# First layer's experts: the last three groups added on TensorE, rows fetched earlier, the branch for left-over rows at the head

## The chip, the cores and the metric

The kernel runs on one core of a Trainium2 chip. The metric is device microseconds of one execution; times are compared as medians of several runs, and the trace is of one further, profiled execution.

## What is computed

Two layers of a small diffusion backbone on 256 context tokens and 256 latent tokens of width 1024. Each layer has a mixer (pooling and differential attention) and then a hierarchical mixture of 32 experts. The change lies in the experts of the first layer, which run over all 512 tokens, and where the second layer's mixer begins. Of the reference that is:

```python
probs_c = jax.nn.softmax(t @ rc_w + rc_b)            # one of four groups for each token
top_v, top_i = lax.top_k(lf, TOP_K_FINE)             # two of its eight experts
gates = einsum('nk,nke->ne', softmax(top_v) * p_group, one_hot(expert_id, N_EXPERTS))
hid = silu(t @ w_gate) * (t @ w_up) * gates          # for each expert
out = sum over the experts of hid @ w_down
x = x + g2 * out                                     # likewise for the context tokens
# the next layer begins with: hx = rmsnorm(x, norm1_g) * (1 + sc1) + sh1;  px = hx @ w_in
```

## The kernel before, in words

**Groups.** A token's row is sent only to its two experts. Experts are sorted by their number of rows, and the sorted list is cut into blocks of 32 rows; four blocks make a group of 128 rows. The first layer has 15 groups, 0 to 14 (`N` and `G` are 15 there). Group 12, 13 and 14 hold four experts each. For every group, `step_apart` runs: `up` (gate and up products, L1445), `turn_hid`, `down` (L1479), and for later groups in between `table` (which rows they take, and a gather of these rows by POOL, L1247) and `turn` (transposes).

**Results of a group.** Group 0 to 12 are "apart" (L1214): the 128 result rows go through `yring` to a table `YD` in memory by a scatter on POOL's queue (L1489). Group 13 and 14 are added on TensorE instead: a selection matrix `P` times the results' high and low parts (`yh`, `yl`; L1529, L1530), one 128 x 512 sum per token tile and half, which `add` multiplies by the gate vector (DVE, L1505) and adds to X (L1507, by DVE and POOL in turn for group 13, by DVE for group 14). The rows in `YD` come back by `fetch` (POOL's queue, L1512, two rows a token, 1 MB a tile) and are added by `add_rows` (three DVE instructions of 128 x 1024, L1517 to L1519). Tiles 0 and 1 are fetched behind group 12, tiles 2 and 3 behind group 13, when the first two have been added.

**Slots and loads.** SBUF has 19 slots of 1 MB (`SB`), used for weights and for large tiles alike. An expert has three loads of 1 MB, issued by SP in one order. Each load in the experts' part takes the slot that `give` hands back when a product has read its weights; `join` takes all slots that lie free into this ring; a load into such a fresh slot is unconditional, every other one is left out by the hardware if the expert has no rows. `lend` hands slots back to `SB` instead. What the next layer loads waits in `pending`; `pump` issues it whenever a slot comes free and more than `keep` stay free. If a request finds no slot, `fill_any` runs a waiting piece of work, here one unit of the modulation matrix of the next layer (`ada_unit`, four matmuls, L414), and takes its slot.

**The branch.** If an expert has more rows than its blocks hold, `left_over` computes them in a loop behind a branch (L1562, L1563). All engines read the flag and branch. Before the change it stands behind group 7. It needs two slots, which `lend` provides. In the runs shown it isn't taken.

**The end of the layer.** `at_end` and `tile_done` begin the next layer's norm for tiles 0 and 1 as their sums are done. The first weight of the next layer has two halves, each split into a high part (ACT) and a low part: the first half's low part by POOL (L500), the second half's by DVE in `mixer`. There `prepare(t)` transposes a tile's rows (L533), scales and splits them (L546 to L551), and the product of each tile follows (L597), copied out by ACT (L599).

## Time and profile before

| | us |
|---|---|
| median of the runs shown | 970.52 (968.68 to 973.1) |
| the profiled execution, its own time | 971.53 |
| its span on the core | 969.7 |
| TensorE matmul busy | 809.7 (84%) |
| VectorE (DVE) busy | 440.9 (45%) |
| ScalarE (ACT) busy | 264.4 (27%) |
| GpSimd (POOL) busy | 189.4 (20%) |
| moved by DMA | 292.91 MB, mean 302 GB/s |

The span is from the first to the last instruction of the trace; what lies around it is 1.8 us here. Matmuls are pipelined, so TensorE's busy time counts overlaps and slow matmuls as busy. Busy time is an average over stages with different limits: the first layer's experts run from some 290 to 590 us, the second layer's mixer follows to some 770, and its experts to the end.

### The profile page before, as it was taken

Reading aid. Unit: us, or ns where it says so; the run is one execution under the profiler, and the core shown is the slowest. Engines: PE = TensorE matmul, PEld = TensorE weight load, DVE = VectorE, ACT = ScalarE, POOL = GpSimd, SP = SyncE. Lnnn points to the kernel's source line nnn. Section 1 sums busy time; section 2 is a strip of 40 time slices with the busy share of each in tenths; the row PEclk is TensorE's granted clock in tenths of the full one; section 3 lists DMA queues with packets and bytes.
Section 4 is the critical chain, followed back from the end, with each engine's and each line's share of the span. In section 5 each row is a group of like instructions: output and inputs, shape, how many; then the busy total and the mean of one; then the engine's idle time right before and its main releaser. Section 6 shows DMA issues by size and latency. Waiting matters only on the chain.

```text
span 969.7 us, 13386 instructions
## 1 busy us (share of the span) xinstructions
PE 809.7 (84%) x4825; PEld 438.2 (45%) x4825; DVE 440.9 (45%) x956; ACT 264.4 (27%) x592; POOL 189.4 (20%) x201
## 2 busy tenths in 40 slices
PE   4799999988995789989866765899878689999873
PEld 1467765654784233333221122677556534443311
DVE  0534405576476222232111078644675734766533
ACT  1632216345350111111000004632572311111101
POOL 1400002234611111111100024000126211222211
PEclk9799999999997889999999887899999789999987
DMA  9988388820729999997999992473227689999992
GB/s 377 417 350 320 130 342 312 332 88 7 303 75 361 369 369 416 416 418 314 410 419 418 408 401 113 179 300 130 97 99 267 249 311 418 418 418 416 418 400 77
DMA packets 49081, 292.91 MB, mean 302 GB/s; under 512 B 7571, under 2 KB 7955, under 8 KB 16880
## 3 DMA queue, kind: packets, MB, share of 16 engines
q1 hardware_dynamic: 36864, 265.74, 68.2%
q0 software_dynamic: 6336, 13.99, 3.8%
q10 hardware_dynamic: 5808, 12.25, 3.4%
q8 instruction: 41, 0.67, 0.3%
q14 instruction: 32, 0.26, 0.1%
HBM read 317.29 MB, written 15.30 MB: 343 GB/s over the span
## 4 chain that ended last, share of the span: by engine, by line
PE 24%; DMA 16%; DVE 6%; ACT 3%; POOL 2%; issue 2%; SPq 0%; POOLq 0%; DVEq 0%; ACTq 0%
DMA we<-in_wx_dram 16%; PE gu L1445 7%; PE dn L1479 5%; PE pj L597 2%; PE pj L467 2%; PE pj L469 2%; PE pj L468 2%; DVE m L1505 1%; PE rowps L414 1%; POOL wl L500 1%; DVE o L1228 1%; POOL wl L464 1%; PE hTp L1264 1%; DVE mx L712 1%; ACT e L718 1%
## 5 line engine op out<-in xcount | busy, mean ns | idle before, releaser
L1479 PE MATMUL dn<-we,t 128*32 128x512 f32 (+2 forms) x672 | 108.5, 639 | 6.5 <-DMA we<-in_wx_dram 4.8
L1451 DVE SCALAR_TENSOR_TENSOR t<-t,tb,gu 128x256 f32<-128x256 f32 x25 | 12.0, 480 | 190.4 <-ACT t L1450 190.4
L1445 PE MATMUL gu<-we,hT0modh 128*32 128x512 f32 (+1 forms) x400 | 62.9, 629 | 10.5 <-DMA we<-in_wx_dram 8.6
L1450 ACT ACTIVATE t<-gu 128x256 f32<-128x256 f32 x25 | 9.6, 384 | 227.0 <-PE gu L1445 227.0
L1445 PE MATMUL gu<-we,hT0modl 128*32 128x512 f32 (+1 forms) x400 | 61.6, 594 | 10.7 <-DMA we<-in_wx_dram 10.1
L1479 PEld LDWEIGHTS dn<-we,t 128*32 128x32 f32 (+2 forms) x672 | 29.5, 122 | 67.6 <-issue 55.0
L414 PE MATMUL rowps<-ada,sT 128*32 128x512 f32 x384 | 54.3, 653 | 5.1 <-DMA ada<-in_adaw_dram 5.1
L1507 POOL TENSOR_TENSOR X<-X,m 128x512 f32<-128x512 f32 x24 | 30.7, 1277 | 142.0 <-DVE m L1505 141.8
L1445 PE MATMUL gu<-we,hT1modl 128*32 128x512 f32 (+1 forms) x272 | 45.6, 652 | 6.1 <-DMA we<-in_wx_dram 6.1
L467 PE MATMUL pj<-hH,wh 128*128 128x512 f32 (+1 forms) x128 | 47.6, 372 | 0.0
L468 PE MATMUL pj<-hL,wh 128*128 128x512 f32 (+1 forms) x128 | 46.5, 363 | 0.0
L469 PE MATMUL pj<-hH,wl 128*128 128x512 f32 (+1 forms) x128 | 46.5, 363 | 0.0
L1507 DVE TENSOR_TENSOR X<-X,m 128x512 f32<-128x512 f32 x32 | 43.6, 1363 | 1.1
L718 ACT ACTIVATE e<-S,nb 128x512 f32<-128x512 f32 (+1 forms) x48 | 29.2, 613 | 46.9 <-DVE nb L715 31.7
L1445 PE MATMUL gu<-we,hT1modh 128*32 128x512 f32 (+1 forms) x272 | 39.5, 622 | 2.4 <-DMA we<-in_wx_dram 1.4
L1247 POOL DMA_INDIRECT h<-hd,ix x14 | 14.3, 1021 | 134.9 <-DVE iy L1254 62.6
L1445 PEld LDWEIGHTS gu<-we,hT0modh 128*32 128x32 f32 (+1 forms) x400 | 17.0, 121 | 52.2 <-issue 35.4
L1445 PEld LDWEIGHTS gu<-we,hT0modl 128*32 128x32 f32 (+1 forms) x400 | 17.0, 115 | 51.1 <-issue 34.2
L712 DVE TENSOR_REDUCE mx<-S 128x1 f32<-128x512 f32 (+1 forms) x48 | 26.8, 596 | 27.7 <-PE S L710 27.6
L1505 DVE TENSOR_TENSOR m<-cb,g 128x512 f32<-128x512 f32 x56 | 36.4, 680 | 0.1
L751 PE MATMUL o<-v,t 128*128 128x128 f32 x160 | 24.5, 293 | 10.3 <-ACT t L739 10.3
L751 PEld LDWEIGHTS o<-v,t 128*128 128x128 f32 x160 | 20.1, 194 | 26.3 <-ACT t L739 23.7
(336 smaller groups left out, 1580.8 us busy)
## 6 DMA issues: line engine op xcount, KB each, us to landing
we<-in_wx_dram SPq DMA_DIRECT2D x207, 1024.0 KB
ada<-in_adaw_dram SPq DMA_DIRECT2D x48, 1024.0 KB
YD<-m ACTq DMA_DIRECT2D x1, 4096.0 KB
yb<-YD POOLq DMA_DIRECT2D x4, 1024.0 KB, 13.5
X<-in_x_dram SPq DMA_DIRECT2D x4, 512.0 KB
e<-in_modb_dram ACTq DMA_DIRECT2D x8, 256.0 KB
band<-in_band_dram SPq DMA_DIRECT2D x2, 1024.0 KB
hd<-h ACTq DMA_DIRECT2D x4, 512.0 KB
```

Of the source, the lines that this page charges most:

```text
L414: pe.matmul(rowps[l][32 * j:32 * j + 32], lhsT=sT[:, k, 4 - 2 * cb:36 - 2 * cb], rhs=h.t[:, 512 * j:512 * j + 512], start=cb < 2 and k == ...
L467: pe.matmul(ps, lhsT=lh, rhs=rh, start=first, stop=False)
L468: pe.matmul(ps, lhsT=lh, rhs=rl, start=False, stop=False)
L469: pe.matmul(ps, lhsT=ll, rhs=rh, start=False, stop=last)
L597: pe.matmul(p.t, lhsT=H[kh].t[:, k, ts], rhs=W3[kh][part].t[:, k], start=n == 0, stop=n == 23)
L712: dve.reduce_max(mx[:, m:m + 1], p.t[:, :nk], axis=AX.X)
L718: act.activation(e[m][:, :nk], S[m].t[:, :nk], AF.Exp, scale=0.125, bias=nb[:, m:m + 1], accum_out=l_[:, m:m + 1])
L751: pe.matmul(o.t[:, h], lhsT=aT[:, kt], rhs=v.t[:, kt, h * 128:h * 128 + 128], start=kt == 0, stop=kt == n - 1)
L1445: pe.matmul(p.t[r], lhsT=hT[k // 4][:, k % 4, r], rhs=gate_up(weights(w, k // 4), k), start=k == 0, stop=k == 7)
L1479: pe.matmul(ps[n2].t[r], lhsT=aT[:, k, r], rhs=down_w(weights(w, 2), k, n2), start=k == 0, stop=k == 1)
L1505: tt(m, q, self.g2[stream(t)][:, ns], op=OP.mult)
L1507: e.tensor_tensor(X[:, t, ns], X[:, t, ns], m, op=OP.add)
```

## The change

The branch `left_over` moves from behind group 7 to the head, ahead of group 0; one slot is kept out of the first `join`, so that it finds two. Group 12 is no longer sent through `YD` but added on TensorE right behind its down product, all by DVE. All four tiles' rows are fetched behind group 11, into three lent slots and `yring`; tiles 0 and 1 are added behind group 12, tiles 2 and 3 behind group 13. The results of groups 13 and 14 are held (`yy`, two slots), and `combine_last` adds both in one sum of four matmuls for each tile and half: tiles 0 and 1 at the layer's end, tiles 2 and 3 inside the next layer's `mixer`, as `late(2)` and `late(3)`. The first half of the next layer's first weight is split ahead of group 14's down product, by ACT and DVE; the second half is copied by ACT ahead of the sums. The loads of the next layer may use every free slot from group 11 on.

```diff
@@ -550,7 +550,7 @@
-    def mixer(l, W3, rows, pre):
+    def mixer(l, W3, rows, pre, late=None):
         last = l == NL - 1
@@ -577,13 +577,15 @@
         else:
-            rests[2]()
+            late(2)
             rests[1](dve)
...
                 prepare(t + 1)
+            if t == 0 and late:
+                late(3)
             if t == 2:
@@ -1203,7 +1205,7 @@
             G = len(groups)
-            tabs, hid, ys, pick = {}, {}, {}, {}
+            tabs, hid, ys, pick, held = {}, {}, {}, {}, []
             hgs = SB.get([128, 2, D], F32, "hg") if near else self.rings.pop(0)
@@ -1211,7 +1213,7 @@
-            apart = lambda g: not near and g < N - 2
+            apart = lambda g: not near and g < N - 3
             rows, back = {}, {}
@@ -1229,7 +1231,7 @@
                 if picked(g):
-                    pick[g] = both[:, 256:].rearrange("p (t s) -> p t s", t=2) if near else w2("e").rearrange("p (t s) -> p t s", t=4)
+                    pick[g] = both[:, 256:].rearrange("p (t s) -> p t s", t=2) if near else yring.t[:, 1, 0:512].rearrange("p (t s) -> p t s", t=4)
                     tt(pick[g], ohs[0][:, :T], ohs[1][:, :T], op=OP.add)
@@ -1364,10 +1366,10 @@
-            def join():
+            def join(left=0):
...
                 hold, SB.after = SB.after, None
-                while SB.slots:
+                while len(SB.slots) > left:
                     h = SB.get([128, 2048], F32, "we")
@@ -1379,7 +1381,7 @@
                 early[0] = 0
-                join()
+                join(1 if N == G else 0)
@@ -1466,8 +1468,9 @@
                 nr = rows_of(g)
+                aside = not near and g >= N - 2
                 if not apart(g):
-                    P = w2("e", F32R)
+                    P = w2("o" if aside and g == N - 2 else "e", F32R)
                     dve.tensor_scalar(P[:nr, :nt], iota512[:nr, :nt], tabs[g][:nr, 6:7], None, op0=OP.is_equal)
@@ -1489,14 +1492,20 @@
                     return
+                for d_ in done:
+                    give(d_, 2)
+                if aside:
+                    hold, SB.after = SB.after, None
+                    if g == N - 2:
+                        hgs.free()
+                    held.append(SB.get([128, 4, 512], F32R, "yy"))
+                    SB.after = hold
                 for n2 in range(2):
-                    yh.append(w2("e", F32R))
-                    yl.append(w2("e", F32R))
+                    yh.append(held[-1].t[:, 2 * n2] if aside else w2("e", F32R))
+                    yl.append(held[-1].t[:, 2 * n2 + 1] if aside else w2("e", F32R))
                     act.activation(yh[n2][:nr], ps[n2].t[:nr], AF.Copy)
...
                     ps[n2].free()
-                for d_ in done:
-                    give(d_, 2)
                 ys[g] = (P, yh, yl)
@@ -1519,7 +1528,7 @@
-            def combine(g, part, tile_done=None):
+            def combine(g, part, tile_done=None, e=None):
                 P, yh, yl = ys[g] if part == 0 else ys.pop(g)
@@ -1528,10 +1537,23 @@
                         pe.matmul(q.t, lhsT=lt, rhs=yl[n2][:nr], start=False, stop=True)
-                        add(q.t, i, n2, None if near or tile_done is None else dve)
+                        add(q.t, i, n2, e)
                         q.free()
...
                         tile_done(i)
+
+            def combine_last(i):
+
+                for n2 in range(2):
+                    q = PS.get([128, 512], F32, "cb")
+                    for n, g in enumerate((N - 2, N - 1)):
+                        P, yh, yl = ys[g]
+                        nr = rows_of(g)
+                        lt = P[:nr, i * 128:i * 128 + 128]
+                        pe.matmul(q.t, lhsT=lt, rhs=yh[n2][:nr], start=n == 0, stop=False)
+                        pe.matmul(q.t, lhsT=lt, rhs=yl[n2][:nr], start=False, stop=n == 1)
+                    add(q.t, i, n2, dve)
+                    q.free()
@@ -1554,9 +1576,6 @@
             gp.dma_start(gv.rearrange("(t p) e -> p t e", p=128), go)
-            room.free()
-            join()
-
             def left_over():
@@ -1609,6 +1628,13 @@
+            hold, SB.after = SB.after, None
+            room.free()
+            if N == G:
+                left_over()
+            SB.after = hold
+            join()
+
             def step_apart(g):
@@ -1637,20 +1663,25 @@
                     turn(g + 1, 1)
+                if g == N - 1 and tail:
+                    tail()
                 down(g)
+                if g == N - 4:
+                    yring.free()
+                    for i in range(T):
+                        fetch(i)
+                    keep[0] = 0
                 if g == N - 3:
-                    for i in range(2):
-                        fetch(i)
-                if g == N - 2:
-                    hgs.free()
                     for part in range(2):
-                        combine(g, part)
+                        combine(g, part, None, dve)
+                    hold, SB.after = SB.after, None
                     for i in range(2):
                         add_rows(i)
+                    SB.after = hold
+                    join()
+                if g == N - 2:
                     for i in range(2, T):
-                        fetch(i)
-                if g == N - 1 and tail:
-                    tail()
+                        add_rows(i)
@@ -1690,31 +1721,33 @@
             for g in range(N):
-                if g == N - 3 and not near:
-                    lend[0] = 2
+                if g == N - 4 and not near:
+                    lend[0] = 3
                 if g == N - 1:
                     keep[0] = 8
-                if g == G // 2 and N == G:
-                    hold, SB.after, lend[0] = SB.after, None, 2
                 if near:
...
                 behind = g
-                if g == G // 2 and N == G:
-                    left_over()
-                    join()
-                    SB.after = hold
-                    if next_loads:
-                        next_loads()
-                        keep[0] = 2
-                        pump()
+                if g == G // 2 and next_loads:
+                    next_loads()
+                    keep[0] = T
             tile_done = at_end() if at_end else None
+            if not near:
+                assert N == G
+                for i in range(2):
+                    combine_last(i)
+                    tile_done(i)
+
+                def late(i):
+                    combine_last(i)
+                    if i == T - 1:
+                        for h in held + [self.gs]:
+                            h.free()
+                return late
             for part in range(2):
                 combine(behind, part, tile_done)
-                if not near and part == 0:
-                    for i in range(2, T):
-                        add_rows(i)
             if N < G:
@@ -1809,30 +1842,27 @@
         rests.append(rest)
-        return first
+        first()
+
+    def tail():
+        start_w3(0)
+        rests[0](dve)
...
         ring = SB.get([128, 2, D], F32, "xn")
-        rests.append(start_w3(1))
-        roots = []
+        start_w3(1)
...
         def tile_done(t):
-            if t < 2:
-                r, root = rms_rows(t, w2("t", BF, [128, D]), later=True)
-                rs.append(r)
-                roots.append(root)
-            if t == 3:
-                rests[0]()
-            if t in (0, 3):
-                return
-            roots[t - 1]()
-            scaled_rows(t - 1, ring, rs[t - 1], True)
-            if t == 2:
+            r, root = rms_rows(t, w2("t", BF, [128, D]), later=True)
+            root()
+            rs.append(r)
+            scaled_rows(t, ring, r, True)
+            if t == 1:
                 rs.append(ring)
...
-    moe.run(next_loads, lambda: start_w3(0)(), at_end)
-    moe = mixer(1, W3, (rs.pop(), dict(enumerate(rs))), {})
+    late = moe.run(next_loads, tail, at_end)
+    moe = mixer(1, W3, (rs.pop(), dict(enumerate(rs))), {}, late)
```

## Rows read from the trace of the kernel before

**Rows 1.** Page, the chain that ended last, share of the span by line.

```profile
DMA we<-in_wx_dram 16%; PE gu L1445 7%; PE dn L1479 5%; PE pj L597 2%; PE pj L467 2%; PE pj L469 2%; PE pj L468 2%; DVE m L1505 1%; PE rowps L414 1%; POOL wl L500 1%; DVE o L1228 1%; POOL wl L464 1%; PE hTp L1264 1%; DVE mx L712 1%; ACT e L718 1%
```

**Rows 2.** One line, the branch: SP waits; ns min/median/max, first to last start.

```profile
L1563 SPq EVENT_SEMAPHORE  x8: 17/17/17, 437.6 to 458.8; - x8
```

**Rows 3.** DMA view from 444 to 464 us: rate in 40 equal slices.

```profile
GB/s 393 426 459 410 410 410 393 426 377 360 361 377 361 344 336 279 295 270 303 254 246 279 270 172 107 16 33 33 49 0 0 115 213 345 418 483 344 459 442 360
```

**Rows 4.** Timeline: start us, us, engine line op out<-in [idle before <- who ended it].

```profile
527.32 0.69 DVE L1484 COPY y<-dn 128x512 f32<-128x512 f32 x1 [6.13 <-PE dn L1479]
...
545.16 0.48 DVE L1451 SCALAR_TENSOR_TENSOR t<-t,tb,gu 128x256 f32<-128x256 f32 x1 [17.15 <-ACT t L1450]
...
568.75 1.21 DVE L1517 TENSOR_TENSOR yb<-yb 128x1024 f32<-128x1024 f32 x1
...
576.59 0.69 PE L1460 MATMUL hdT<-cst,t 128*128 128x128 f32 x2 [7.51 <-DVE t L1451]
...
577.81 6.72 PE L1479 MATMUL dn<-we,t 128*32 128x512 f32 x32 [0.53 <-ACT t L1462]
...
587.85 0.69 DVE L1507 TENSOR_TENSOR X<-X,m 128x512 f32<-128x512 f32 x1
```

**Rows 5.** Stretches: us, busy us by engine, clock granted, DMA share, GB/s.

```profile
557.00:584.00 27.00, 18.70 (x115) 6.77 (x114) 19.06 (x22) 1.96 (x4) 6.58 (x6) 0.87 1.00 400
584.00:616.00 32.00, 17.21 (x62) 11.55 (x61) 29.21 (x41) 16.91 (x31) 12.20 (x10) 0.73 0.29 107
```

**Rows 6.** Timeline of the second layer's start.

```profile
593.53 1.37 PE L533 MATMUL xTp<-cst,xn 128*128 128x128 f32 x8 [4.34 <-ACT xn L523]
...
614.56 0.60 ACT L599 ACTIVATE v<-pj 128x512 f32<-128x512 f32 x1 [0.52 <-PE pj L597]
...
636.34 0.60 ACT L599 ACTIVATE v<-pj 128x512 f32<-128x512 f32 x1 [6.06 <-PE pj L597]
```

**Rows 7.** Waits of SP from 290 to 330: us in total, times, longest.

```profile
SPq L1015 <- DMA gv<-rt: 8.0, 1, 8.0
```

**Rows 8.** DMA view from 300 to 340 us: rate in 40 equal slices.

```profile
GB/s 422 430 381 410 434 418 455 410 410 283 12 0 156 344 434 418 418 418 426 434 422 426 406 434 410 418 418 393 82 74 188 401 401 352 311 381 381 447 422 426
```

**Rows 9.** Timeline: first matmuls at the head, and behind the branch at group 7.

```profile
306.85 3.65 PE L1445 MATMUL gu<-we,hT0modh 128*64 128x512 f32 x16 [0.69 <-ACT hT0modh L1272]
...
433.33 3.64 PE L1445 MATMUL gu<-we,hT0modh 128*32 128x512 f32 x32 [1.08 <-DVEq L1563]
```

**Rows 10.** DMA view from 543 to 555: queue, packets, MB, share of 16 engines.

```profile
q1 hardware_dynamic: 445, 3.24, 65.3%
q0 software_dynamic: 448, 1.77, 36.4%
```

**Rows 11.** Groups of instructions from 552 to 637: count, busy us, mean ns.

```profile
L1505 DVE TENSOR_TENSOR m<-cb,g 128x512 f32<-128x512 f32 x16 | 10.6, 679 | 0.0
...
L1529 PE MATMUL cb<-e,e 128*128 128x512 f32 x16 | 6.7, 418 | 0.1
...
L546 DVE TENSOR_SCALAR e<-xTp,col 128x128 f32<-128x128 f32 x16 | 5.5, 403 | 2.6 <-PE xTp L533 2.6
L551 DVE TENSOR_TENSOR hL<-e,hH 128x512 fp32r<-128x512 f32 x8 | 5.3, 688 | 1.7 <-ACT hH L550 1.6
...
L500 DVE TENSOR_TENSOR wl<-('win', 1)_131_4712,wh 128x512 fp32r<-128x512 f32 x4 | 2.5, 686 | 0.0
...
L525 DVE TENSOR_SCALAR xn<-X,rs 128x1024 f32<-128x1024 f32 x2 | 1.5, 745 | 0.0
```

**Rows 12.** Timeline of SP: the last group's weight loads.

```profile
535.75 24.29 SPq L1015 DMA_DIRECT2D we<-in_wx_dram  x12
```

**Rows 13.** DMA view from 543 to 592: the weight queue.

```profile
q1 hardware_dynamic: 1895, 13.73, 69.2%
```

**Rows 14.** Timeline of SP: a load for the next layer.

```profile
568.68 0.33 SPq L308 DMA_DIRECT2D ('win', 1)_137_4796<-in_win_dram  x1
```

**Rows 15.** Waits of SP from 545 to 600.

```profile
SPq L308 <- DMA we<-in_wx_dram: 5.2, 3, 2.1
```

## The prediction

> **What bounds the kernel now.** I read the page's chain first, then the stretch from the first layer's experts to the second layer's first products, because every line of the change lies there. The longest link of the chain is the experts' weight stream [rows 1]. So a change in the first layer's experts pays in two ways only: the stream ends earlier, or less work follows between its end and the second layer.
>
> The stream has one hole that it makes itself. After the branch at the middle group, SP, which issues all weight loads, passes eight semaphore waits from 437.6 to 458.8 us [rows 2], one after another: it lets every load under way land before it issues the next. The transfer rate sinks from 449 us, is near zero at 456 and back at 461 [rows 3]. The 40 slices of half a microsecond have a mean of 291 GB/s; a full slice has about 418, at which a load of 1.05 MB takes 2.5 us. So the hole is 20 x (1 - 291/418) = 6.1 us.
>
> Behind the stream the bound changes to DVE. The last group's gate-and-up matmuls end at 569.1, but TensorE then idles 7.51 us for the multiply behind them, because DVE first adds group 13's sums and, from 568.75, the fetched rows of two tiles; its next 32 matmuls take 6.72 us [rows 4]. From 584 to 616 DVE is busy 29.2 of 32 us and TensorE has a granted clock of 0.73 [rows 5]: adds, then the rows of tiles 2 and 3 (six instructions like that at 568.75, 7.3 us or more), then the splits of the first product. The product of the first tile is copied out at 614.56, the fourth at 636.34, 7.3 us a tile [rows 6].
>
> **The change part by part.** The sum goes against the profiled execution, 971.5 us (span 969.7); that is 1.0 above the median 970.5 of the runs shown.
>
> *Branch to the head.* The hole of 6.1 us at group 7 goes; bounds 0 (it returns elsewhere) and 6.1. At the head SP again waits for all loads under way, but it stands still there anyway: for 8.0 us until the gate table `gv` has landed [rows 7], with nothing moving at 311 to 312 [rows 8]. Since `join(1)` keeps back one slot, one load of 2.5 us fewer is under way before the branch, and the kept slot is loaded right behind it instead of with `gv`; I put the loads at 0. All five engines read the flag and branch. The nearest row is the same branch at group 7, where TensorE idles 1.08 us for DVE's passing; at the head the first matmuls start at 306.85 [rows 9]. Bounds 0 (the flags are read while the engines drain) and 3 (one engine after the other); I take 0.7, near that row. That delay reaches the stream at 328 to 331, where it stands still until the first down product frees slots [rows 8]. Net -5.4.
>
> *Rows fetched behind group 11, all four.* Today two fetches (1.05 MB each) lie ahead of the last weights and two behind; then all four lie ahead: 2.1 MB at 418 GB/s, +5.0 us. While a fetch runs it takes 1.77 of 5.01 MB, the weights keep 3.24 [rows 10]. POOL waits for group 11's scatter before the fetches; behind that wait in its queue stand the gather of group 14 and nothing that is due soon. *Group 12 added on TensorE.* Its scatter of 0.52 MB goes: -1.25. Its 16 matmuls and 16 DVE instructions (0.68 + 0.69 us a pair, so 11 us) and two tiles' rows (6 x 1.22 = 7.3) [rows 4, 11] come on DVE between group 12's copy, which ends at 528.0 today, and group 13's multiply at 545.16 [rows 4]: 18.3 us of work in 17.2, a space that grows while fetches slow the weights in it. Cost 0; without that cover 1.1, and more if a fetched row lands late.
>
> *An extra load.* The last group's 12 loads are issued between 535.75 and 559.96 [rows 12], seven loads for the next layer follow, and yet from 543 on the weight queue moves only 13.7 MB, 13.1 loads [rows 13]: at least six of the twelve move nothing. They are conditional, and the last two experts are empty. The new `join` behind group 12 fills two slots unconditionally; by my count of slots these are the first weights of the last group's second and third expert, and the third is empty: +2.5.
>
> Sum for the stream: -5.4 + 5.0 - 1.25 + 2.5 = +0.85. Three of the next layer's loads waited for the landing of expert loads, the last until 568.68 [rows 14, 15]: so the last down weights land at 568.6 today, then at 569.5. The stream gains nothing; what it wins at the branch it pays out again.
>
> *Group 14 without DVE in front.* With groups 13 and 14 in one sum, the adds of 13 go, and the rows of tiles 2 and 3 (7.3 us) run behind group 13's down product, ready at about 565. The last gate-and-up matmuls end when their weights allow, some 568; multiply, transpose and copy 2 us; the down product starts at 570.4 and takes 3.6 (warm) to 6.7 us (cold) [rows 4]: 574 to 577. The split of the next layer's first weight is put ahead of this on ACT and DVE (2.5 us on DVE [rows 11], behind ACT's copies one by one); it needs a load that lands 2.5 us behind the last down weights, 572, so DVE comes to the group's low parts at 575.5. Then 2 x 0.7 and four adding instructions of 0.69: tile 0 is done at 579.7, today 588.5 [rows 4]: -8.8.
>
> *A new wait on TensorE.* Counting slots: at the second layer's start 19 are taken by two `yy`, `gs`, `xn`, one raw weight, four split ones, six loaded ones and the layer's first four; its fifth request finds none, and `fill_any` runs one unit of the modulation matrix, whose slot it frees. That stands on TensorE ahead of the second layer's first transposes and must wait for its load, the seventh behind the last expert weights: 569.5 + 7 x 2.5 = 587. The transposes would be ready at about 584 (579.7 and at most the 5.0 us that lie between the two today [rows 4, 6]). They start at 588.3, today 593.53 [rows 6]: -5.2 instead of -8.8.
>
> *Second layer's first products.* Between the transposes and the fourth product lie 42.8 us today. Then DVE has, from 590: multiply-adds 1.4, low part 1.4, tile 2's sum 2.75, the second weight's split 2.5, again 1.4 and 1.4, tile 3's sum 2.75, scaled rows 0.75 [rows 11]: 604.3; the rows' 7.3 us are gone. TensorE has transposes 1.4 [rows 6], 16 matmuls of the two late sums (6.7 us at most [rows 11]; they overlap, I take 5), then transposes and the first product, 7.3 as for a tile today: 602, and waits for DVE until 604.3. Three more tiles at 7.1 to 7.3 us: 626. Today 636.34: -10.5. Behind that nothing is changed, and the transfer engines have room (107 GB/s from 584 to 616 [rows 5]), so the gain should stay to the end: **971.5 - 10.5 = 961**.
>
> A rule of the Trainium skill speaks against the new wait. The row: between 584 and 616, where TensorE stands still most of the time, the granted clock is 0.73 [rows 5], so between the levels 1.2 and 2.4 GHz, and the down product behind 7 idle us took 6.72 us [rows 4]. The skill ("TensorE: Matmul & The Clock Gate", Part 1) says that the throttled state is the default and only activity lifts it. By that rule the late sums and transposes start at the low level, and the trace agrees; priced from rows it is up to 3 us, of which the sum holds about half.
>
> **The rivals.** *The wait doesn't bind* (the modulation load lands before the transposes, or the stream ends earlier because the clashes of fetch and weights cost less): the front end keeps its -8.8 and the DVE list the rest, -15: 956. For it: DVE and ACT alone would allow 584. Against: seven loads in a row behind the last weights can't move faster than 418 GB/s.
>
> *The hole only moves.* SP's wait for all loads costs 6.1 us at the head as it did at group 7; then the stream ends 6 us later than I say, and all behind it: 967. For it: the same eight waits are in the program. Against: SP stands still at the head already.
>
> *Nothing arrives:* DVE's list in the second layer, or a wait that I don't see there, eats what the front wins: 971.
>
> *Slower: the modulation unit on TensorE.* In program order it is ahead of everything in the second layer. If the stream (hole moved +6, fetches slower than 418 GB/s would have it +5) ends 11 us later, the unit waits until 598, and the gain is gone; every further us costs one. With 5 us more: 976. It decides from a landing of the modulation load at 598 on. Against it: two fetches at a time cost the weights no more than their bytes [rows 10].
>
> **How the numbers follow.** Chances: forecast 0.43, wait doesn't bind 0.18, hole moves 0.17, nothing arrives 0.11, slower 0.11. 0.5% is 4.9 us, about what a measurement of this kernel can tell from no change; counted from the median, faster is below 965.7. The forecast and the first rival are faster, and a small part of the second: 0.64. Within 0.5%: 0.25. Slower by more: 0.11. Range: unknown terms are the branch at the head (0 to +6), the clock at the down product (0 to 3), the extra load (-2.5 if both experts are full), the wait (-5); 951 to 970, which leaves out the slower case and the ends.
>
> **What would show it.** Right: no fall of the rate near 456; SP's eight waits near 305 and the loads going on by 312; the last group's multiply within 1 us of its ACT step; a unit of L414 (one modulation matmul group) on TensorE ahead of the first transposes, idle time before it ended by a load; the fourth product copied out near 626. Wrong: a hole at 310 of more than 4 us, group 13's multiply waiting for DVE, or the transposes waiting for ACT alone.

## The result and the profile after

| | before | changed |
|---|---|---|
| median of the runs on one chip, us | 970.19 (968.68 to 973.10, 4 runs) | 960.61 (959.67 to 961.47, 4 runs) |
| the same on a second chip, us | 969.42 (11 runs) | 960.50 (6 runs) |
| ratio, first chip | 1 | 0.9889, 95% interval 0.9862 to 0.9917 |
| profiled execution, us (span) | 971.5 (969.7) | 960.6 (958.8) |

The change makes the kernel 9.6 us faster, 1.1%. The forecast was 961 (951 to 970). The following lines are of the changed kernel's first profile. First the page: its chain by line, the group of the modulation matmuls (L414), and the fetches.

```profile
DMA we<-in_wx_dram 23%; PE gu L1447 8%; PE dn L1482 5%; DMA ada<-in_adaw_dram 2%; PE pj L599 2%; PE pj L467 2%; PE pj L468 2%; PE pj L469 2%; DMA h<-hd,ix 1%; DVE m L1514 1%; DVE o L1230 1%; PE rowps L414 1%; PE hTp L1268 1%; DVE X L1516 1%; PE hTp L1266 1%
...
L414 PE MATMUL rowps<-ada,sT 128*32 128x512 f32 x384 | 54.7, 658 | 13.7 <-DMA ada<-in_adaw_dram 13.7
...
yb<-YD POOLq DMA_DIRECT2D x4, 1024.0 KB, 22.5
```

The weight stream has a larger share of the chain than in [rows 1], and a new link stands in it: a load of the modulation matrix (`ada`). Then the two stretches that held the branch, as rates in 40 slices: 444 to 464 us (answering [rows 3]) and 300 to 340 us (answering [rows 8]), and SP's waits from 300 to 340 (answering [rows 7]).

```profile
GB/s 393 442 377 475 410 393 426 377 418 442 426 418 393 402 434 426 410 393 418 434 475 369 442 410 459 410 426 393 426 442 426 426 410 360 442 377 401 401 401 418
```

```profile
GB/s 418 418 426 447 373 475 406 279 82 8 139 213 410 401 418 442 401 418 442 426 418 406 438 410 418 418 418 442 360 66 98 287 442 385 319 348 360 406 451 401
```

```profile
SPq L1582 <- SPq L1582: 2.5, 3, 1.7
SPq L1017 <- DMA gv<-rt: 0.4, 1, 0.4
```

And the branch's own semaphore waits (answering [rows 2]):

```profile
L1582 SPq EVENT_SEMAPHORE  x8: 17/17/17, 306.7 to 309.1; - x8
```

The hole at 456 is gone: the slices from 444 to 464 have a mean of 416 GB/s instead of 291. At the head SP passes the eight waits in 2.4 us instead of 21, and five slices lie well below the full rate, from 307 on where it was from 309; what they lack of 418 GB/s is 3.3 us against 3.1. The queue now stands there for its own loads (2.5 us) and hardly for the gate table, 0.4 us where it was 8.0. Last the tail, as a timeline (answering [rows 4, 6, 14]) and by stretches (answering [rows 5]).

```profile
570.50 0.48 DVE L1453 SCALAR_TENSOR_TENSOR t<-t,tb,gu 128x256 f32<-128x256 f32 x1 [4.29 <-ACT t L1452]
571.41 0.33 SPq L308 DMA_DIRECT2D ('win', 1)_140_4803<-in_win_dram  x1
572.01 5.38 PE L1482 MATMUL dn<-we,t 128*32 128x512 f32 x32 [0.53 <-ACT t L1464]
...
580.72 0.69 DVE L1516 TENSOR_TENSOR X<-X,m 128x512 f32<-128x512 f32 x1
...
588.84 1.94 PE L414 MATMUL rowps<-ada,sT 128*32 128x512 f32 x8 [7.47 <-DMA ada<-in_adaw_dram]
590.70 1.97 PE L533 MATMUL xTp<-cst,xn 128*128 128x128 f32 x8
...
606.58 1.09 PE L533 MATMUL xTp<-cst,xn 128*128 128x128 f32 x8 [2.83 <-DVE xn L525]
...
627.36 0.60 ACT L601 ACTIVATE v<-pj 128x512 f32<-128x512 f32 x1 [6.07 <-PE pj L599]
```

```profile
557.00:584.00 27.00, 19.99 (x116) 6.68 (x112) 17.81 (x24) 8.24 (x16) 0.81 (x2) 0.94 1.00 406
584.00:616.00 32.00, 24.34 (x117) 18.12 (x118) 20.14 (x40) 17.86 (x36) 3.07 (x6) 0.84 0.33 115
```

The last group's multiply follows its ACT step at once. DVE's work from 584 to 616 fell from 29.2 to 20.1 us, as the fetched rows of tiles 2 and 3 are added before. The modulation unit stands ahead of the first transposes and TensorE waits 7.47 us for its load. The fourth product comes 9.0 us earlier (627.36 against 636.34). Of the 11.0 us by which the two profiled executions differ, 1.2 more is the unit itself: it no longer stands in the products of the next weights, which begin 9.0 us earlier and end 10.2 us earlier. From the fourth product to the attention's first matmul it is 50.52 us in every profile in which a unit ran ahead of the transposes, and 51.75 in every one in which none did, the kernel before included. The rest, under 1 us, comes later.

### The profile page after: what moved, and what is told of

It is laid out like the page before. It is cut to its first block, busy times and chain, and to the rows that moved or that the text cites. A ratio compares the mean times of both kernels' runs of the same rounds, so it can differ in the third digit from the quotient of the medians.

```text
span 958.8 us, 13409 instructions
## 1 busy us (share of the span) xinstructions
PE 814.8 (85%) x4841; PEld 442.2 (46%) x4841; DVE 441.7 (46%) x965; ACT 265.8 (28%) x593; POOL 174.1 (18%) x192
## 3 DMA queue, kind: packets, MB, share of 16 engines
q1 hardware_dynamic: 37008, 266.78, 69.3%
## 4 chain that ended last, share of the span: by engine, by line
PE 27%; DMA 26%; DVE 7%; ACT 2%; issue 1%; POOL 1%; SPq 0%; POOLq 0%; DVEq 0%; ACTq 0%
DMA we<-in_wx_dram 23%; PE gu L1447 8%; PE dn L1482 5%; DMA ada<-in_adaw_dram 2%; PE pj L599 2%; PE pj L467 2%; PE pj L468 2%; PE pj L469 2%; DMA h<-hd,ix 1%; DVE m L1514 1%; DVE o L1230 1%; PE rowps L414 1%; PE hTp L1268 1%; DVE X L1516 1%; PE hTp L1266 1%
## 5 line engine op out<-in xcount | busy, mean ns | idle before, releaser
L1447 PE MATMUL gu<-we,hT0modl 128*32 128x512 f32 (+1 forms) x400 | 66.0, 631 | 10.8 <-DMA we<-in_wx_dram 10.1
L414 PE MATMUL rowps<-ada,sT 128*32 128x512 f32 x384 | 54.7, 658 | 13.7 <-DMA ada<-in_adaw_dram 13.7
L1447 PE MATMUL gu<-we,hT1modl 128*32 128x512 f32 (+1 forms) x272 | 42.6, 604 | 5.5 <-DMA we<-in_wx_dram 5.5
L1516 POOL TENSOR_TENSOR X<-X,m 128x512 f32<-128x512 f32 x20 | 25.6, 1278 | 117.5 <-DVE m L1514 117.3
L1447 PEld LDWEIGHTS gu<-we,hT0modl 128*32 128x32 f32 (+1 forms) x400 | 17.8, 121 | 54.7 <-issue 36.5
L720 ACT ACTIVATE e<-S,nb 128x512 f32<-128x512 f32 (+1 forms) x48 | 29.2, 613 | 46.7 <-DVE nb L717 31.5
L1447 PEld LDWEIGHTS gu<-we,hT0modh 128*32 128x32 f32 (+1 forms) x400 | 16.9, 120 | 49.4 <-issue 36.5
L753 PE MATMUL o<-v,t 128*128 128x128 f32 x160 | 24.5, 293 | 10.1 <-ACT t L741 10.1
L753 PEld LDWEIGHTS o<-v,t 128*128 128x128 f32 x160 | 20.1, 194 | 26.2 <-ACT t L741 23.6
```

What stands on the lines that cost most here:

```text
L414: pe.matmul(rowps[l][32 * j:32 * j + 32], lhsT=sT[:, k, 4 - 2 * cb:36 - 2 * cb], rhs=h.t[:, 512 * j:512 * j + 512], start=cb < 2 and k == ...
L720: act.activation(e[m][:, :nk], S[m].t[:, :nk], AF.Exp, scale=0.125, bias=nb[:, m:m + 1], accum_out=l_[:, m:m + 1])
L753: pe.matmul(o.t[:, h], lhsT=aT[:, kt], rhs=v.t[:, kt, h * 128:h * 128 + 128], start=kt == 0, stop=kt == n - 1)
L1447: pe.matmul(p.t[r], lhsT=hT[k // 4][:, k % 4, r], rhs=gate_up(weights(w, k // 4), k), start=k == 0, stop=k == 7)
L1516: e.tensor_tensor(X[:, t, ns], X[:, t, ns], m, op=OP.add)
```

## The experiments

The theory is the prediction's: the expert stream ends the first layer, the hole counts nearly in full, and the unit's load then holds TensorE. The main rival is that VectorE's list (DVE) sets the second layer's start whatever the stream and TensorE do. The first experts' matmuls (`gu`) start at 306.85 before, at 307.53 and 306.70 in two profiles of the changed kernel, and between 305.7 and 307.9 in all others but one (310.9). So the stream is measured from there, and the tail, up to the fourth product copied out, from the end of the last gate-and-up matmuls. That the last needed expert weights have landed is read from SP: the load for the next layer that takes the slot released by them starts then.

**The branch alone, on the kernel before.**

```diff
-                join()
+                join(1 if N == G else 0)
...
+            room.free()
+            if N == G:
+                left_over()
...
-                if g == G // 2 and N == G:
-                    left_over()
-                    join()
```

> The kernel before with the branch for rows left over moved to the head of the groups and nothing else changed. Theory (the hole of 6.1 us counts in full and the head is nearly free): the stream runs through 440 to 461, the last group's down weights land near 562.5 instead of 568.6, everything behind moves with them, 964 against 970. Rival (the head pays it back, or the work on VectorE behind the stream hides it): 969 to 970, with a new standstill of about 6 us near 310 or the same 7.5 us of TensorE waiting for VectorE grown to 13.

The edit also moves the place of one small table (`pick`), as the change does. Measured: 966.9 against 969.6, ratio 0.9974 (0.9950 to 0.9999). One line of SP, two of TensorE and one of ACT; then the kernel before's line for the first of the two:

```profile
546.26 6.42 PE L1479 MATMUL dn<-we,t 128*32 128x512 f32 x26 [2.71 <-DMA we<-in_wx_dram]
...
562.70 0.33 SPq L308 DMA_DIRECT2D ('win', 1)_135_4793<-in_win_dram  x1
571.84 0.69 PE L1460 MATMUL hdT<-cst,t 128*128 128x128 f32 x2 [7.51 <-DVE t L1451]
...
631.59 0.60 ACT L599 ACTIVATE v<-pj 128x512 f32<-128x512 f32 x1 [6.06 <-PE pj L597]
```

```profile
552.10 5.32 PE L1479 MATMUL dn<-we,t 128*32 128x512 f32 x26 [2.74 <-DMA we<-in_wx_dram]
```

TensorE's wait for DVE is 7.51 us as in [rows 4], not 13; everything behind the stream moved 4.7 to 4.8 us (fourth product 631.59 against 636.34). But the first experts' matmuls began 1.2 us earlier in this execution, as the first layer's attention had done. Counted from them, the last weights come 4.8 us sooner than before and all that follows only 3.6: group 13's down product, started by its weights, took 6.42 us instead of 5.32 at a granted clock of 0.56 instead of 0.68, and group 14's matmuls stood behind it, not behind their weights. The median moved 2.7 us, and its interval reaches from 0.1 to 4.8 us. The mechanism is the theory's; its price is 4.8 us in the stream, not 6, and on this kernel less at the end.

**The branch put back, on the changed kernel.**

```diff
-                join(1 if N == G else 0)
+                join()
...
-            if N == G:
-                left_over()
             SB.after = hold
             join()
...
+                if g == G // 2 and N == G:
+                    hold, SB.after, lend[0] = SB.after, None, 2
...
+                if g == G // 2 and N == G:
+                    left_over()
+                    join()
```

> The changed kernel with the branch put back behind group 7, all else as changed. Theory (stream and the modulation unit on TensorE decide the tail): the hole returns, the modulation load and with it the second layer's first transposes come 5.5 to 6 us later, 966.5 against 960.6. Rival (VectorE and ScalarE decide the second layer's first products, the stream has slack behind the last expert): under 3 us, 961 to 963.

Measured: 966.0, ratio to the kernel before 0.9961 (0.9944 to 0.9978). The rate from 444 to 464, and the same line of SP:

```profile
GB/s 328 475 360 434 483 311 442 352 385 361 352 353 336 295 336 254 279 270 279 279 246 197 131 57 33 16 33 33 0 0 147 197 320 311 434 426 459 377 377 459
...
574.44 0.33 SPq L308 DMA_DIRECT2D ('win', 1)_142_4805<-in_win_dram  x1
```

The hole returns, and from the first experts' matmuls on the last weights land 4.4 and 5.2 us later than in the two profiles of the changed kernel. The tail is unchanged (58.9 us; changed 57.3 and 58.9), and the end moves by 5.4 us (960.6 to 966.0, two chips). So the branch is worth 4.4 to 5.4 us in the changed kernel, and the rest of the change 3.6 us beside the kernel before on the same chip (969.6).

**No branch at all.**

```diff
             room.free()
-            if N == G:
-                left_over()
             SB.after = hold
```

> The changed kernel without the first layer's branch for rows left over (with this case's data it isn't taken, so nothing that counts is left out). Prices the branch at the head by itself. The prediction's value: 0.7 us, first experts' matmuls 0.7 us earlier and all behind it too, 960. By the balance of the runs so far (the hole of 6.1 us came through as 4.6): 1.5 us, last down weights at 568.3 instead of 569.8, 959. Rival (the eight waits cost at the head what they cost at group 7): 5 to 6 us, 955.

Measured: 960.05, ratio 0.9908 (0.9887 to 0.9930), against 0.9892 (0.9870 to 0.9915) for the changed kernel on another chip. No gain, and the last weights land at 569.90, 264 us behind the first experts' matmuls, as in the changed kernel (263 to 264 in its two profiles). That count leaves out a later start of these matmuls; they start 159.1 us behind the first layer's first attention matmul here, and 159.1 and 160.2 in the changed kernel. At the head the branch costs nothing that can be measured; 1.5 and the rival's 5 to 6 fall, and 0.7 was too much.

**The modulation unit taken away from the transposes.**

```diff
                 if g == N - 1:
-                    keep[0] = 8
+                    keep[0] = 8 if near else 9
```

> The changed kernel, where the last group leaves nine slots free for the next layer instead of eight, so that no modulation unit runs ahead of the second layer's first transposes. Theory (TensorE stands there for the unit's load): the transposes start near 585.5 instead of 590.7, the fourth product is copied out 4 us earlier, 956.5 against 960.6. Rival (VectorE's list decides the fourth product whenever the transposes start): 0 to 1 us, 960.

Measured: 959.79, ratio 0.9894 (0.9871 to 0.9917); the changed kernel has 0.9892. Transposes of tiles 0 and 2, and the second and fourth product copied out; then the stretch 604 to 610 of this kernel and, in a fence of its own, of the changed one:

```profile
585.49 1.09 PE L533 MATMUL xTp<-cst,xn 128*128 128x128 f32 x8 [3.46 <-ACT xn L523]
...
603.11 1.97 PE L533 MATMUL xTp<-cst,xn 128*128 128x128 f32 x8 [5.49 <-DVE xn L525]
...
611.84 0.60 ACT L601 ACTIVATE v<-pj 128x512 f32<-128x512 f32 x1 [2.60 <-PE pj L599]
626.01 0.60 ACT L601 ACTIVATE v<-pj 128x512 f32<-128x512 f32 x1 [6.06 <-PE pj L599]
...
604.00:610.00 6.00, 6.00 (x23) 4.97 (x22) 4.85 (x10) 4.85 (x10) 0.54 (x1) 0.70 0.30 123
```

```profile
604.00:610.00 6.00, 3.42 (x19) 3.00 (x20) 4.38 (x9) 4.23 (x10) 0.79 (x2) 1.00 0.62 220
```

The changed kernel has two profiles: in the first the transposes start 20.7 us behind the last gate-and-up matmul, tile 2's 36.5, and the tail is 57.3; in the second 20.7, 36.5 and 58.9. Here, where that matmul ends at 570.7, they are 14.8, 32.4 and 55.3. So the transposes come 5.9 us earlier, as the theory says; tile 2's 4.1, since they wait for DVE to scale the rows (L525); the fourth product 2.0 to 3.5. TensorE idles 5.49 us ahead of tile 2 instead of 2.83 in the first profile, the granted clock from 604 to 610 is 0.70 instead of 1.00, and the eight transposes take 1.97 us instead of 1.09. In the second profile, where it idled 3.8 us, that clock is 0.72, and it is this profile whose tail is 1.5 us longer. So the wait on TensorE was real, but about half of it went to DVE's order and to the low level of the clock. Of the rest 1.2 us is paid later: the unit now stands among the next weights' products, 51.75 us from the fourth product to the attention instead of 50.52. In the medians nothing of it is resolved (0.7 us less than 960.5, ratios 0.9894 and 0.9892; single runs 958.3 to 964.0). The profile is of the slowest of these runs, 964.03: its last weights came 1.7 to 2.4 us later than the changed kernel's, counted from the first experts' matmuls, and its second attention was slow (last section). The Trainium skill ("TensorE: Matmul & The Clock Gate", Part 1) calls the throttled state the default, which activity lifts; the 0.70 and 0.72 behind 5.49 and 3.8 idle us and the 1.00 behind 2.83 agree.

**VectorE's order.** Where DVE's list is the bound, its order is a lever: the rows of tile 2 are scaled ahead of tile 3's late sums, those of tile 3 ahead of the next weight's split. Two kernels ran beside the changed one, the second with the unit gone as well.

```diff
                 if t > 1 and not late:
                     scaled_rows(t, ring, rs[t])
...
             if t == 0 and late:
+                scaled_rows(2, ring, rs[2])
                 late(3)
+            if t == 1 and late:
+                scaled_rows(3, ring, rs[3])
```

> The changed kernel once more, as the measure for the others that run beside it on this chip: 960.6, and against the kernel before 0.989.

> The changed kernel, where the second layer's start scales the rows of tile 2 ahead of the late sums of tile 3 on VectorE, and those of tile 3 ahead of the next weight's split. Theory (VectorE's order sets tile 2's transposes, and TensorE's idle time there is all that the unit's removal could not win): tile 2's transposes at 604 instead of 606.6, fourth product copied out at 624.8 instead of 627.4, 958. Rival (the fourth product hangs on VectorE's whole list, not on its order): the third or fourth product waits instead, 960.6.

> The same order of VectorE's work, and in addition nine slots left free so that no modulation unit stands ahead of the second layer's first transposes. Theory: the transposes at 585.5, first product copied out at 598.9, tile 2's transposes at 600 to 601 with TensorE idle under 2.5 us and its clock not falling, fourth product 621 to 623, 954.5. Rival (the stream's end and the clock eat it again): fourth product at 626, 959.

Measured on one chip: 960.50 for the changed kernel, 957.19 for the order alone (ratio to before 0.9876, 0.9842 to 0.9909), 956.71 with the unit gone too (0.9857, 0.9834 to 0.9880). Tile 2's transposes and the fourth product of the order alone, then of both with the stretch 604 to 610:

```profile
602.78 1.09 PE L533 MATMUL xTp<-cst,xn 128*128 128x128 f32 x8 [1.21 <-DVE xn L525]
...
623.93 0.60 ACT L604 ACTIVATE v<-pj 128x512 f32<-128x512 f32 x1 [6.07 <-PE pj L602]
```

```profile
598.12 1.09 PE L533 MATMUL xTp<-cst,xn 128*128 128x128 f32 x8 [2.31 <-DVE xn L525]
...
619.28 0.60 ACT L604 ACTIVATE v<-pj 128x512 f32<-128x512 f32 x1 [6.06 <-PE pj L602]
...
604.00:610.00 6.00, 5.69 (x34) 3.85 (x33) 6.00 (x12) 5.40 (x12) 0.00 (x0) 1.00 0.18 33
```

Both theories hold up to here: the tail is 54.9 us with the order, 51.2 with both (57.3 and 58.9 changed), and behind tile 2's wait the clock doesn't fall. Taking the unit away is worth 2.0 to 3.5 us without the order and 3.7 with it. At the end the order keeps 3.3 us by the medians, though with one run of six at 965.06 its interval overlaps that of the changed kernel; with the unit gone too all five runs (955.5 to 957.9) lie below every run of the changed kernel (958.4 to 962.1). Of the second gain 0.5 us is left in the medians, which isn't resolved. In the profiles 1.2 us of its 3.7 go to the unit in its later place (51.75 against 50.52 us again), and 2.5 in the second layer's attention (last section).

**The load of the empty expert.** The last group holds the experts that stand at 24, 25, 30 and 31 in the list sorted by rows; the last two have none.

```diff
+            if not near:
+                m, n = todo.index((30, 0)), todo.index((24, 1))
+                todo[m], todo[n] = todo[n], todo[m]
```

> The changed kernel, where two entries of the list of loads change places, so that the two slots that join behind group 12 take weights of experts that have rows and the unconditional load of the empty third expert of the last group is gone. Theory (that load is 2.5 us of the stream): the last down weights land at 568.8 instead of 571.3, the second layer's first transposes at 588.2 instead of 590.7. At the end: 2.5 us less, 958, if TensorE's start decides; 0 to 1 us less, as where the transposes started 5 us earlier, if VectorE's list and the clock behind it decide.

Measured: 960.15, ratio 0.9881 (0.9850 to 0.9913), beside 960.50. Last weights, here and in the changed kernel's second profile:

```profile
567.86 0.33 SPq L308 DMA_DIRECT2D ('win', 1)_140_4803<-in_win_dram  x1
```

```profile
569.84 0.33 SPq L308 DMA_DIRECT2D ('win', 1)_140_4803<-in_win_dram  x1
```

2.0 us earlier, with the same tail (58.9), so the fourth product is copied out 1.9 us earlier (625.38); a load costs about what its bytes say. That this load was the change's extra one is seen in the bytes: over the whole execution the weight queue moves 265.74 MB before, 266.78 changed and 265.74 here. In the medians 0.35 us of it is seen, less than the runs scatter (955.1 to 964.0).

**The weight queue behind VectorE's adds.** The trace of the changed kernel showed a wait that the prediction didn't have: two loads take the slots of fetched rows, so SP, and every load behind them, stands until DVE has added those rows. SP's wait in the changed kernel from 536 to 562:

```profile
SPq L1017 <- DVE X L1528: 6.0, 2, 3.1
```

In the second profile it is 7.3 us. Does it cost anything? Rows added earlier:

```diff
+                if g == N - 3:
...
+                    for i in range(2):
+                        add_rows(i)
...
+                    join()
                 down(g)
...
                         combine(g, part, None, dve)
...
-                    for i in range(2):
-                        add_rows(i)
...
-                    join()
```

> The changed kernel with the fetched rows of tiles 0 and 1 added ahead of group 12's down product instead of behind its sums, so that their slots join earlier; one unconditional load of an empty expert is still among the loads. Theory A (the weight queue standing 6 us for VectorE's adds at 544 to 551 costs the stream what the mean rate lost there, about 2 us): last weights near 569.5, 958.7 against 960.6. Theory B (each load's last sixteenth lands every 2.5 us without a pause from 544 to 571, so the slowest of the transfer engines never stood still): 960.6, no change. If group 12's down product now waits for VectorE, it is slower than 961.

Measured: 962.50, ratio 0.9928 (0.9905 to 0.9951). The wait is gone from SP, and the last weights land at 569.95, as at 569.84 in the changed kernel's second profile: theory B. All stages to the fourth product agree within 0.2 us. The profiled executions differ by 0.1 us (spans 959.6 and 959.5). Why the median is 2 us above the changed kernel's, on another chip, stays open.

**The price of the fetches.** Two of the four fetches left out, first with the adds where they are, then with them early.

```diff
+                if i < 2:
                     gp.dma_start(back[i].t, YD.rearrange("(k t p) d -> t p k d", k=2, p=128)[i])
```

> The changed kernel without fetching and adding the rows of tiles 2 and 3 (two of the four fetches, 2.1 MB; the slots are still taken and given back), which leaves their first twelve groups out of the sum, so only the time up to the second layer's first products is read. Theory (a fetch costs the stream its bytes at 418 GB/s): last down weights 5.0 us earlier, 564.8 instead of 569.8. Rival (a fetch runs beside the weights and costs little, or its small packets cost more than their bytes): under 3 us, or over 6.

> As half_rows (the rows of tiles 2 and 3 are neither fetched nor added, so only the time up to the second layer's first products is read), with the rows of tiles 0 and 1 added ahead of group 12's down product, so that the weight queue doesn't stand for VectorE's adds. Where that queue took the gain of two fetches less (last down weights 567.3, not 564.8): now 564.8 to 565.5. If a fetch really costs the stream only half its bytes: 567.3 again.

SP's waits from 530 to 556 and its line of the last weights in the first, and that line in the second:

```profile
SPq L1017 <- DVE X L1530: 10.1, 2, 7.0
...
567.31 0.33 SPq L308 DMA_DIRECT2D ('win', 1)_140_4795<-in_win_dram  x1
```

```profile
565.61 0.33 SPq L308 DMA_DIRECT2D ('win', 1)_140_4795<-in_win_dram  x1
```

With less to move, SP's wait for DVE grows to 10.1 us and takes part of the gain: 1.9 us from the first experts' matmuls on, not 5. With the wait gone too it is 4.8 us against the early rows alone. The whole times of these two kernels, 2216 and 2207 us, say nothing here: with rows missing from the sum, the loop for left-over rows runs in the second layer, with 192 loads of 1 MB of its own by the page. So 2.1 MB cost the weights the 5.0 us of their bytes, and the wait for DVE stands just behind the stream, hidden by it.

**All three together:** order, unit and empty load.

> All three together: VectorE's order in the second layer's start, no unit ahead of the transposes, no load of the empty expert. Theory (each gain passes on because none of the others stands behind it any more): last down weights at 567.8, transposes at 581, fourth product copied out at 617.3 against 619.3 with the load and 627.3 in the changed kernel, 954.5. Rival (next in line is the next layer's weights, which land behind the last expert): fourth product at 619, 956.7.

Measured: 956.16 (949.86 to 958.19), ratio 0.9848 (0.9821 to 0.9874). It beats both kernels: 13.2 us below before, and 4.3 below the changed kernel's 960.5 (another chip). In its profile the first experts start 4.2 us late, because the first layer's attention was slow in that execution (its score matmuls span 86.3 us instead of 80.8); from there the last weights come after 260.9 us (changed: 263.1 and 263.9), and the tail is 51.1 us, as without this edit. That is the theory's gain up to that point. Against the version without this edit, 0.5 us in the medians, it isn't resolved.

## Why the prediction was right, step by step

| step | predicted | first profile | second profile |
|---|---|---|---|
| branch: hole less head | -5.4 | -4.4 to -5.2 by the two branch kernels | |
| two more fetches ahead | +5.0 | +4.8 | |
| load of the empty expert | +2.5 | +2.0 | |
| last down weights land | 569.5 | 571.4 | 569.8 |
| last down product starts | 570.4 | 572.0 | 570.4 |
| tile 0 done | 579.7 | 581.4 | 579.8 |
| unit's matmuls / transposes start | 587 / 588.3 | 588.8 / 590.7 | 587.3 / 589.1 |
| fourth product copied out | 626 | 627.4 | 627.3 |
| total | 961 | 960.6 | 961.3 |

*Branch.* The step was right, with its terms off in both directions: the head, put at 0.7, costs about 0, and the hole, put at 6.1, 4.4 to 5.2. The slices of [rows 3] lie below the full rate from 449 on, but not all that they lack was lost to the last weights. Where the other us was made good was not tried. How much reaches the end differs too: 5.4 us in the changed kernel, 2.7 in the kernel before.

*Stream.* The sum of +0.85 was measured as +1.3 to +2.1 from the first experts' matmuls on (before 261.8, changed 263.1 and 263.9). Everything but the branch was put at +6.25 and comes to +6.5 (268.3 with the branch put back). Its two tested positive terms were right within 0.5 us; the scatter's -1.25 wasn't tried alone, and what 6.5 leaves for it beside 4.8 and 2.1 is -0.4, a difference of single profiles. The 18.3 us of DVE work in 17.2 just fit in the first profile, where group 13's multiply started right behind it at 550.5 and its ACT step had ended at 550.48. In the second the multiply came 1.3 us behind its ACT step and TensorE idled 1.67 us for it instead of 0.41, which is one of the prediction's signs of being wrong. It cost nothing at the end: with the rows added early that wait is gone (0.41 us), group 13's down product waits for its weights instead, and the last weights land at 569.95, not before 569.84. That step also overlooked that SP stands behind the same adds, 6.0 us, because their slots take the next loads. By the same kernel it cost the stream nothing.

*Group 14.* Right, given when the weights landed: in the second profile the down product's start and tile 0 are within 0.1 us of the forecast.

*New wait on TensorE.* It is there with its predicted load, place and time. The transposes came 0.8 to 2.4 us later than forecast: the unit started 0.3 and 1.8 us late, and it takes 1.94 us, not the 1.0 to 1.3 that 587 and 588.3 allowed, at or near the low level of the clock, 1.2 GHz (granted share from 586 to 592: 0.50 and 0.57).

*Second layer.* The forecast of DVE as the one for which TensorE waits was right: its list up to tile 2's scaled rows (L525) was put at 16.0 us from the first transposes and took 15.8 in both profiles, so it ended at 606.5 and 604.9 instead of 604.3. The fourth product is 1.3 us late, and a term was missing that made it good: the unit done early leaves 1.2 us free later. The mechanism was right, but that 960.6 meets 961 so closely is in part luck: the late fourth product and the missing term cancel, as do in part the hole that was priced too high and the head's 0.7.

*Rivals.* "The wait doesn't bind" was the one with a wrong price. The kernel without the unit is that rival, made: 959.8, not 956. Its sum let the whole front-end gain through, without asking whether DVE's order would be next, what TensorE's longer idle time does to its clock, and where the unit goes instead (1.2 us later). With the order mended, 956.7 was measured. "The hole only moves" fell with the kernel that has no branch, "nothing arrives" (971) with the measured 960.6, and the slower case with the unit's load landing at 588.8 at the latest, nine us ahead of the 598 from which it decides.

## What to carry to other kernels

In this kernel a branch that is not taken still made the queue that issues the loads wait for all that it had under way; put such a branch where that queue stands anyway. When two bounds lie close together, removing the first shows almost nothing: price the second from the same trace, here the order of DVE's list, and change both. Work that is taken out of one place is paid in another: count it there, as with the unit's 1.2 us. A slot that is handed from one use to the next ties the queue of its next load to the engine that frees it, here SP to DVE for 6.0 us; list these waits for any step that you move.

## What the runs showed of the hardware that I had not expected

The parts of one load do not land together. In the changed kernel's second profile fifteen of the sixteen parts of the last down weights are in by 566.9, the sixteenth at 569.8; its later loads repeat the gap. In the kernel with two fetches less and SP waiting 10.1 us, all sixteen land by 567.2, 0.3 us behind the fifteenth. In the changed kernel the sixteenth parts of the loads landed every 2.4 to 2.7 us from 547 to 570, straight through SP's wait of 7.3 us, while the first fourteen parts paused from 549.7 to 551.0. So that pause cost the stream nothing, and the mean rate, which falls in it, overstates what is lost: from 515 to 556 it is 375 GB/s, and 400 with the rows added early, with the last weights at 569.84 and 569.95. The Trainium skill ("DMA: Bandwidth & Descriptors", "Why a DMA increments its semaphore by 16 and not by 1") says that a transfer's engines finish independently; the 2.9 us show by how much here. What delays the one is open.

The same instructions of the second layer's attention take 1 to 3 us more in some executions. From the attention's first matmul to the second layer's first expert it is 90.5 to 91.9 us in ten profiles and 92.7 to 93.8 in four (unit gone; order and unit; empty load gone; two fetches less). These four show a granted clock of 0.83 from 670 to 700, the other changed kernels 0.89 or 0.94, and the same over the 30 us from the attention's first matmul. The row of the changed kernel, then that of the kernel without the unit:

```profile
670.00:700.00 30.00, 26.79 (x132) 17.73 (x130) 19.13 (x38) 17.31 (x43) 5.12 (x5) 0.94 0.37 132
```

```profile
670.00:700.00 30.00, 27.00 (x118) 17.63 (x116) 15.62 (x29) 16.68 (x40) 5.13 (x5) 0.83 0.33 116
```

Such a slip is as large as the gains that were tested; what sets it off was not found.
